# Ten pairs of feed-forward blocks as two-by-two block products with seven multiplications, summed in HBM

## The chip, the cores and the metric

One core of one Trainium2 chip runs the kernel. Its engines are PE (TensorE, the matrix products), DVE (VectorE), ACT (ScalarE), POOL (GpSimd) and SP (SyncE, which here only issues DMAs); each works through its own list of instructions in order and waits on semaphores. PE reads from SBUF and writes into PSUM, which has eight banks of 128 x 512 floats here. The metric is the device time of one launch in microseconds. Before the change it is 2099.76 us, the median of three runs that lie between 2098.71 and 2101.66 us.

## The reference, cut to what matters

The layer holds 1024 tokens of 1024 features, in float32:

```python
x = LN1(ALPHA * x + 0.5 * swiglu(x, f1_gate, f1_up, f1_down))     # feed-forward 1
x = LN2(ALPHA * x + token_mixer(x))                               # gated delta rule and gated linear attention
x = LN3(ALPHA * x + 0.5 * swiglu(x, f2_gate, f2_up, f2_down))     # feed-forward 2

def swiglu(x, w_gate, w_up, w_down):        # 1024 -> 2816 -> 1024
    return (silu(x @ w_gate) * (x @ w_up)) @ w_down
```

The inner width 2816 makes 22 blocks of 128 features in each feed-forward part. The change concerns ten of the 2 x 11 pairs of such blocks.

## The kernel before, in words

Every float32 operand is kept as two parts, hi and lo (`split`, lines 119 to 121: ACT rounds to hi, DVE subtracts and stores lo), and every product is three matrix products: hi hi, hi lo, lo hi. So a product of a 128 x 128 piece of weights with 512 tokens costs three MATMULs of 512 columns each. Tokens lie transposed in SBUF as tiles `xh` and `xl` [features, tokens], eight per half of the tokens.

The work of a block of 128 features, for one half of 512 tokens: `gate_silu` and `up` (both through `proj`, lines 176 to 187) each run 24 MATMULs into one bank `pa` (8 tiles of features times 3). ACT takes silu of the first, DVE multiplies it with the second, and `split` makes the parts of the hidden values. `down` (lines 189 to 211) multiplies the hidden values of two blocks with the rows of w_down: 6 MATMULs into a bank `pd`, then one DVE instruction (line 210) adds the bank to `acc`, the running sum of the layer in SBUF, which starts as x.

Weights come through `weight`: SP loads 128 x 512 (256 KB) into a raw tile `wr` (5 buffers), and ACT and DVE split it into `wh` and `wl` (6 buffers each). The raw loads run ahead as buffers come free.

The order: feed-forward 1, blocks 0 to 11, both halves of the tokens (`ffn_groups`); then the middle, where the remaining ten blocks of feed-forward 1 and the first eight of feed-forward 2 (one half of the tokens at a time) are fed by a hand-written table (`pull`) between the small steps of the mixer, so that PE always has work; then blocks 8 to 21 of feed-forward 2, both halves, the last four of them half by half with the last layer norm behind them. DMAs are issued by SP alone; POOL only raises to a power and clears tiles.

## Time and profile before

| what | value |
|---|---|
| time, median of three runs | 2099.76 us (2098.71 to 2101.66) |
| span of the profiled execution, first to last instruction | 2097.4 us, so some 2.4 us lie around it |
| granted TensorE clock, mean | 0.999 of full |
| PE busy | 2067.7 us, 99% of the span, 10292 instructions |
| DVE busy | 1284.9 us, 61% |
| ACT busy | 697.2 us, 33% |
| POOL busy | 54.6 us, 3% |
| moved by DMA | 163.03 MB, mean 78 GB/s |

The page gives for each engine its busy time and the number of its instructions; a MATMUL's busy time is its length from issue to the modelled end, and MATMULs overlap, so busy time over count is not the time that one of them adds to the span. A group row gives line, engine, operation, output <- inputs, shapes and count, then total busy time, the mean of one, and the idle time of the engine before them with what ended it. A windows row gives for a stretch of the span the busy time and count of each engine, the granted clock, the share of time in which the 16 DMA engines moved data, and the rate.

### The profile page before, as it was taken

How to read it: one execution, taken by the hardware profiler on the slowest of the kernel's cores; microseconds unless marked ns; L12 is line 12 of the kernel's file. 1: busy time of each engine (PE TensorE's matmuls, PEld its weight loads, DVE VectorE, ACT ScalarE, POOL GpSimd, SP SyncE). 2: the span in 40 equal slices, each digit the busy share in tenths (PEclk: the TensorE clock that was granted, in tenths of full speed). 3: DMA queues.
4: the chain of work that ended last, by engine and by line, in shares of the span. 5: the costliest groups of instructions: out<-in, count | busy, mean ns of one | idle time of the engine just before them, and what ended most of it. 6: DMA issues, size and time to landing. Idle time of an engine off the chain costs nothing.

```text
span 2097.4 us, 27456 instructions
## 1 busy us (share of the span) xinstructions
PE 2067.7 (99%) x10292; PEld 1695.0 (81%) x10292; DVE 1284.9 (61%) x2793; ACT 697.2 (33%) x1395; POOL 54.6 (3%) x87
## 2 busy tenths in 40 slices
PE   9999999999999999999999999999999999999998
PEld 7888888888887787788788777888788888888887
DVE  4434333454678888768899887778755333333456
ACT  5211121123254444434464443343422211112232
POOL 0000000000000000000101000001000000000000
PEclk9999999999999999999999999999999999999999
DMA  8111111122222212222131222122323211111232
GB/s 288 49 55 48 43 55 46 46 97 99 89 93 86 71 56 79 70 69 91 66 111 66 71 76 66 66 71 71 121 96 105 80 46 46 51 40 61 76 106 85
DMA packets 87109, 163.03 MB, mean 78 GB/s; under 512 B 10048, under 2 KB 10560, under 8 KB 86976
## 3 DMA queue, kind: packets, MB, share of 16 engines
q1 hardware_dynamic: 86976, 161.29, 22.9%
q8 instruction: 80, 1.31, 0.3%
q14 instruction: 53, 0.43, 0.1%
HBM read 157.06 MB, written 4.19 MB: 77 GB/s over the span
## 4 chain that ended last, share of the span: by engine, by line
PE 87%; DVE 8%; ACT 2%; issue 2%; POOL 1%; DMA 1%; SPq 0%; DVEq 0%; ACTq 0%; POOLq 0%
PE pa L183 17%; PE pa L184 17%; PE pa L186 17%; PE pd L205 8%; PE pd L206 8%; PE pd L207 8%; PE pm L824 1%; PE pm L422 1%; DVE wl L121 1%; DVE acc L210 1%; DVE acc L264 1%; PE pa L724 1%; DVE xl L121 1%; PE pa L725 1%; PE pa L723 1%
## 5 line engine op out<-in xcount | busy, mean ns | idle before, releaser
L183 PE MATMUL pa<-xh,wh 128*128 128x512 f32 x1808 | 716.6, 397 | 8.7 <-ACT xh L120 5.1
L184 PE MATMUL pa<-xl,wh 128*128 128x512 f32 x1808 | 708.7, 392 | 0.1
L186 PE MATMUL pa<-xh,wl 128*128 128x512 f32 x1792 | 704.3, 393 | 0.0
L121 DVE TENSOR_TENSOR wl<-wr,wh 128x512 fp32r<-128x512 f32 (+1 forms) x489 | 334.1, 686 | 350.9 <-ACT wh L120 340.9
L120 ACT CAST wh<-wr 128x512 fp32r<-128x512 f32 (+1 forms) x489 | 302.6, 621 | 709.5 <-PE pa L184 482.9
L183 PEld LDWEIGHTS pa<-xh,wh 128*128 128x128 f32 x1808 | 340.5, 188 | 80.0 <-ACT xh L120 5.9
L184 PEld LDWEIGHTS pa<-xl,wh 128*128 128x128 f32 x1808 | 340.3, 188 | 68.0 <-DVE xl L121 1.8
L186 PEld LDWEIGHTS pa<-xh,wl 128*128 128x128 f32 x1792 | 337.2, 188 | 67.9
L210 DVE SCALAR_TENSOR_TENSOR acc<-pd,acc 128x512 f32<-128x512 f32 x433 | 293.8, 687 | 125.4 <-PE pd L207 122.0
L205 PE MATMUL pd<-wh,hh 128*128 128x512 f32 x416 | 165.4, 404 | 2.2 <-ACT xf L254 1.4
L206 PE MATMUL pd<-wl,hh 128*128 128x512 f32 x416 | 164.2, 396 | 0.1
L207 PE MATMUL pd<-wh,hl 128*128 128x512 f32 x416 | 162.1, 395 | 0.0
L319 DVE TENSOR_TENSOR xf<-xf,pa 128x512 f32<-128x512 f32 x88 | 60.4, 686 | 165.8 <-PE pa L186 165.8
L206 PE MATMUL pd<-fl,gh 128*128 128x512 f32 (+1 forms) x386 | 150.0, 389 | 0.0
L205 PE MATMUL pd<-fh,gh 128*128 128x512 f32 (+1 forms) x386 | 150.0, 389 | 0.0
L207 PE MATMUL pd<-fh,gl 128*128 128x512 f32 (+1 forms) x386 | 149.8, 388 | 0.0
L205 PEld LDWEIGHTS pd<-wh,hh 128*128 128x128 f32 x416 | 78.1, 188 | 24.2 <-ACT hh L120 5.1
L120 ACT CAST fh<-wr 128x512 fp32r<-128x512 f32 x52 | 32.2, 622 | 195.4 <-PE pd L207 165.6
L207 PEld LDWEIGHTS pd<-wh,hl 128*128 128x128 f32 x416 | 78.1, 188 | 17.7 <-DVE hl L121 2.9
L206 PEld LDWEIGHTS pd<-wl,hh 128*128 128x128 f32 x416 | 78.3, 188 | 13.9 <-DVE wl L121 0.8
L205 PEld LDWEIGHTS pd<-fh,gh 128*128 128x128 f32 x386 | 72.5, 188 | 15.2
L207 PEld LDWEIGHTS pd<-fh,gl 128*128 128x128 f32 x386 | 72.5, 188 | 15.2
(251 smaller groups left out, 1987.5 us busy)
## 6 DMA issues: line engine op xcount, KB each, us to landing
wr<-gu SPq DMA_DIRECT2D x263, 256.0 KB, 2.5
wr<-wd SPq DMA_DIRECT2D x132, 256.0 KB, 2.6
wr<-win SPq DMA_DIRECT2D x116, 256.0 KB, 2.6
wr<-wout SPq DMA_DIRECT2D x32, 256.0 KB, 2.5
acc<-xT SPq DMA_DIRECT2D x16, 256.0 KB, 5.4
acc<-x SPq DMA_DIRECT2D x8, 512.0 KB, 8.7
out_dram<-acc SPq DMA_DIRECT2D x7, 512.0 KB, 2.6
g<-lnrow SPq DMA_DIRECT2D x9, 256.0 KB, 3.4
```

The source lines that it names most:

```text
L120: self.nc.scalar.copy(hi, src)
L121: self.nc.vector.tensor_tensor(lo, src, hi.bitcast(F32), ALU.subtract)
L183: nc.tensor.matmul(ps[:], hi[:, sl], xh[k][:], start=(k == 0), stop=False)
L184: nc.tensor.matmul(ps[:], hi[:, sl], xl[k][:], start=False, stop=(lo is None and k == KB - 1))
L186: nc.tensor.matmul(ps[:], lo[:, sl], xh[k][:], start=False, stop=(k == KB - 1))
L205: nc.tensor.matmul(p, hh[:, sl], wh[:, ds], start=(i == 0), stop=False)
L206: nc.tensor.matmul(p, hh[:, sl], wl[:, ds], start=False, stop=False)
L207: nc.tensor.matmul(p, hl[:, sl], wh[:, ds], start=False, stop=(i == n - 1))
L210: nc.vector.scalar_tensor_tensor(acc, p, scale / ALPHA, acc, ALU.mult, ALU.add, accum_out=None if sums is None else sums[:, d:d + 1])
L264: nc.vector.tensor_tensor(acc, acc, g[:], ALU.mult)
L319: self.nc.vector.tensor_tensor(s[:], s[:], ps[:], ALU.mult)
L422: self.nc.tensor.transpose(self.chunk(ps, c), s, self.ident)
```

## The change

Two blocks of features are taken together and all 1024 tokens at once, so that gate, up and down are each a product of matrices cut into two-by-two blocks. Such a product is formed from seven block products instead of eight (with the fewest additions: four sums on each of the two operand sides, and sums of results). In the diff P1 and P2 use plain blocks, P4 uses one plain and one summed block, P3 one summed token block and a plain weight block, and P5, P6, P7 use sums on both sides. Blocks 2 to 11 of feed-forward 1 (five pairs) and blocks 8 to 17 of feed-forward 2 (five pairs) go this way.

- `token_sums` makes the four sums of the tokens once for each chain of five pairs; `weight_sums` makes four sums of the weights for every step (gate, up or down of a pair). Sums are DVE instructions, and each of the seven operands of a step is split into hi and lo.
- `project` runs gate or up: seven products of 12 MATMULs, in two banks that each go on adding; banks that are needed later as partial sums are copied to SBUF by ACT (`keep`).
- `down_sums` runs down: seven products of four tiles of tokens, 12 MATMULs each, in all eight banks. The results don't go to `acc`: ACT copies a bank to a tile `ev` (7 buffers), for P2 and P7 DVE adds the second bank to it, and POOL issues a DMA that adds the tile to the running sum `accd`, which lies in HBM (`add_out`). Twenty such DMAs of 256 KB leave each down step; `out=True` gives `down` the same way out.
- The steps follow each other as gate of pair n+1, down of pair n, up of pair n+1. Weights are prepared four to five products ahead (`DEEP`).
- Because the sum lies in HBM while these chains run, x is first copied there, and `acc` is loaded before the middle, stored behind it and loaded again before the last four blocks. Room in SBUF is given out by phase. The second half of the tokens of blocks 0 to 7 of feed-forward 2 has moved from the end of the middle into the phase behind it, with its sums in HBM too.

On PE there are 8867 rows before and 8507 now, 360 fewer. In the rows below names end in the numbers of their buffers; L595 is ACT's copy of a bank into `ev`, L138 the cast that gives a hi part (`wh` for weights), L510 the copy of a bank in `keep`, L197 POOL's adding DMA, L587 to L589 the products of down, L542 the first product of gate or up. DMASW and DMAHW name landings of POOL's and of SP's DMAs.

DVE, in a down step before: banks are added to the sums in SBUF, and each waits for PE alone.

```order
L210 SCALAR_TENSOR_TENSOR acc0_9_91<-pd_316_1775,acc0_9_91 128x512 [waits PE_49]
L210 SCALAR_TENSOR_TENSOR acc0_9_91<-pd_317_1783,acc0_9_91 128x512 [waits PE_49]
L210 SCALAR_TENSOR_TENSOR acc1_16_110<-pd_318_1791,acc1_16_110 128x512 [waits PE_49]
L210 SCALAR_TENSOR_TENSOR acc1_16_110<-pd_319_1799,acc1_16_110 128x512 [waits PE_49]
L210 SCALAR_TENSOR_TENSOR acc2_21_121<-pd_320_1807,acc2_21_121 128x512 [waits PE_49]
```

ACT now, at the end of a down step (the last tile of P3, then P4's four) and the start of the up step behind it:

```order
L595 ACTIVATE ev_481_1980<-pm_469_1918 128x512 [waits DMASW4_49,DVE_49,PE_49]
L138 CAST wh_488_2012<-wr_471_1924 128x512
L595 ACTIVATE ev_484_1990<-pa_439_1811 128x512 [waits DMASW5_49,DVE_49,PE_49]
L595 ACTIVATE ev_485_1996<-pa_441_1817 128x512 [waits DMASW6_49,DVE_49,PE_49]
L595 ACTIVATE ev_486_2002<-pm_443_1823 128x512 [waits DMASW7_49,DVE_49,PE_49]
L595 ACTIVATE ev_487_2008<-pm_445_1829 128x512 [waits DMASW0_49,PE_49,Activation_49]
L138 CAST wh_492_2031<-wr_472_1926 128x512 [waits DMAHW2_49]
L138 CAST wh_497_2055<-wr_460_1894 128x512 [waits PE_49]
L510 COPY sn_491_2029<-pa_490_2016 128x512 [waits PE_49]
```

Emptying a bank has moved from DVE to ACT, and it now also waits until an earlier adding DMA has landed, since only then is an `ev` tile free. The casts of weights stand behind it in ACT's list.

PE now, at the same place: the last tile of P4, then P1 of the up step.

```order
L587 MATMUL pm_445_1829<-wh_453_1864,xh12_389_1593 128x512 [waits DVE_49]
L588 MATMUL pm_445_1829<-wl_454_1865,xh12_389_1593 128x512
L589 MATMUL pm_445_1829<-wh_453_1864,xl12_390_1594 128x512
L542 MATMUL pa_490_2016<-xh00_7_91,wh_461_1896 128x512 [waits Activation_49]
L543 MATMUL pa_490_2016<-xl00_8_92,wh_461_1896 128x512
L544 MATMUL pa_490_2016<-xh00_7_91,wl_462_1897 128x512
```

P1 of the up step waits for ACT, which has to empty the bank `pa` that P4 filled.

The diff, cut to its core:

```diff
-BUFS = {"w": 6, "h": 3, "xf": 3, "wr": 5, "f": 4, "g": 6, "raw": 1, "q": 1, "k": 2, "v": 1, "tt": 1, "z": 1, "on": 2, "am": 1, "pt": 1, "qd": 1, "vb": 1,
+BUFS = {"w": 6, "h": 3, "xf": 3, "wr": 7, "f": 4, "g": 6, "gs": 4, "sn": 4, "ev": 7, "raw": 1, "q": 1, "k": 2, "v": 1, "tt": 1, "z": 1, "on": 2, "am": 1, "pt": 1, "qd": 1, "vb": 1,
+PRODUCTS = (("P1", 0), ("P2", 1), ("P6", 0), ("P5", 1), ("P7", 0), ("P3", 1), ("P4", 0))
+DEEP = 4
...
+    def load_acc(self, pool):
+        for c in range(KB):
+            self.acc[c] = self.wt(pool, [D], f"acc{c}", 1)
+            self.nc.sync.dma_start(self.acc[c][:], self.accd[c][:])
+    def add_out(self, t, c, d):
+        self.nc.gpsimd.dma_start(self.accd[c][:, HALVES[d]], t[:], accum_op=ALU.add)
...
             for p, (c, d, cut) in zip(ps, now):
+                if out:
+                    t = self.u("ev", self.fx)
+                    nc.scalar.activation(t[:], p, AF.Copy, scale=scale / ALPHA)
+                    self.add_out(t, 4 * half + c, d)
+                    continue
...
+    def token_sums(self, src):
+        tt = self.nc.vector.tensor_tensor
+        self.sx = {n: [] for n in ("P5", "P6", "P7", "P3")}
+        for q in range(KB // 2):
+            a = {}
+            for i, j in ((1, 0), (1, 1), (0, 0), (0, 1)):
+                a[i, j] = self.stage()
+                self.nc.sync.dma_start(a[i, j][:], src(i, 4 * j + q))
+            s1, s2 = self.stage(), self.stage()
+            tt(s1[:], a[1, 0][:], a[1, 1][:], ALU.add)
+            tt(s2[:], s1[:], a[0, 0][:], ALU.subtract)
+            tt(a[0, 0][:], a[0, 0][:], a[1, 0][:], ALU.subtract)
+            tt(a[0, 1][:], a[0, 1][:], s2[:], ALU.subtract)
+            for n, t in (("P6", s2), ("P5", s1), ("P7", a[0, 0]), ("P3", a[0, 1])):
+                hl = [self.wt(self.fx, [HT], f"s{n}{q}{e}", 1, F32R) for e in "hl"]
+                self.split(hl[0][:], hl[1][:], t[:])
+                self.sx[n].append(hl)
...
+    def weight_sums(self, b11, b12, b21, b22):
...
+        t11, t21 = load(b11), load(b21)
+        yield parts(t11)
+        t12, t22 = load(b12), load(b22)
+        yield parts(t21)
+        t2 = self.u("wr", self.wp)
+        tt(t11[:], t12[:], t11[:], ALU.subtract)
+        tt(t2[:], t22[:], t11[:], ALU.subtract)
+        yield parts(t2)
+        yield parts(t11)
+        tt(t12[:], t22[:], t12[:], ALU.subtract)
+        yield parts(t12)
+        yield parts(t22)
+        tt(t21[:], t21[:], t2[:], ALU.subtract)
+        yield parts(t21)
+    def project(self, hid, up):
...
+        for n, b in PRODUCTS:
+            op = yield
+            if n in ("P1", "P2", "P5"):
+                banks[b] = self.bank("pd" if b else "pa")
+            ps = banks[b]
+            for q, (xh, xl) in enumerate(self.tokens(n)):
+                sl = slice(q * P, (q + 1) * P)
+                new = n in ("P1", "P2", "P5") and q == 0
+                nc.tensor.matmul(ps[:], op[0][:, sl], xh[:], start=new, stop=False, skip_group_check=True)
+                nc.tensor.matmul(ps[:], op[0][:, sl], xl[:], start=False, stop=False, skip_group_check=True)
+                nc.tensor.matmul(ps[:], op[1][:, sl], xh[:], start=False, stop=q == 3, skip_group_check=True)
+            if n in ("P1", "P6", "P5"):
+                keep(n, ps)
+            elif n == "P2":
+                done("11", (kept["P1"], ps))
+            elif n == "P7":
+                done("22", (kept["P5"], ps))
+            elif n == "P3":
+                done("12", (kept["P6"], ps))
+            else:
+                done("21", None)
+        if up:
+            s1, s2 = self.u("sn", self.fx), self.u("sn", self.fx)
+            tt(s1[:], hid["21"][:], hid["22"][:], ALU.add)
+            tt(s2[:], s1[:], hid["11"][:], ALU.subtract)
+            tt(hid["21"][:], hid["11"][:], hid["21"][:], ALU.subtract)
+            tt(hid["12"][:], hid["12"][:], s2[:], ALU.subtract)
+            for n, t in (("P6", s2), ("P5", s1), ("P7", hid["21"]), ("P3", hid["12"])):
+                self.hidden_part(hid, n, t)
...
+    def down_sums(self, hid, scale):
+        nc = self.nc
+        tags = ("pa", "pa", "pm", "pm"), ("pd", "pd", "pd", "pm")
+        banks = [[None] * 4, [None] * 4]
+        ev = {}
+        for n, b in PRODUCTS:
+            op = yield
+            hh, hl = hid[n]
+            new = n in ("P1", "P2", "P5")
             for c in range(4):
+                if new:
+                    banks[b][c] = self.bank(tags[b][c])
+                ps, sl = banks[b][c], slice(c * P, (c + 1) * P)
+                nc.tensor.matmul(ps[:], hh[:, sl], op[0][:], start=new, stop=False, skip_group_check=True)
+                nc.tensor.matmul(ps[:], hh[:, sl], op[1][:], start=False, stop=False, skip_group_check=True)
+                nc.tensor.matmul(ps[:], hl[:, sl], op[0][:], start=False, stop=True, skip_group_check=True)
+                if n in ("P2", "P7"):
+                    t = ev[c]
+                    nc.vector.scalar_tensor_tensor(t[:], ps[:], scale, t[:], ALU.mult, ALU.add)
+                else:
+                    t = ev[c] = self.u("ev", self.fx)
+                    nc.scalar.activation(t[:], ps[:], AF.Copy, scale=scale)
+                if n in ("P2", "P6", "P7", "P3", "P4"):
+                    i, j = {"P2": (0, 0), "P6": (0, 1), "P7": (1, 1), "P3": (0, 1), "P4": (1, 0)}[n]
+                    self.add_out(t, 4 * i + c, j)
...
     def run(self):
...
-        self.ffn_groups(1, [range(n, n + 2) for n in range(0, K1, 2)], first=True)
-        with self.tc.tile_pool(name="mp", bufs=1) as self.mp:
-            self.middle()
-        cut = [*range(K2, NF - LAST, 2), NF - LAST]
-        self.ffn_groups(2, [range(a, b) for a, b in zip(cut, cut[1:])], last=range(NF - LAST, NF))
+        self.staged = 0
+        with self.phase("fa") as self.fx:
+            self.scr = "gs", self.fx
+            self.first_pair()
+            self.load_constants()
+            self.token_sums(lambda half, k: self.a["xT"][half, k])
+            self.ffn_pairs(1, range(2, K1))
+        with self.phase("ap") as ap:
+            self.load_acc(ap)
+            with self.phase("hp") as self.hp, self.phase("sp") as self.sp, self.phase("mp") as self.mp:
+                self.scr = "xf", self.hp
+                for k in range(KB // 2):
+                    self.restore(1, k)
+                self.middle()
+            for c in range(KB):
+                self.spill(c, self.acc[c][:])
+        with self.phase("fb") as self.fx:
+            self.scr = "gs", self.fx
+            now(self.ffn(2, range(K2), 1, True))
+            self.token_sums(lambda half, k: self.x2d[half, k][:])
+            self.ffn_pairs(2, range(K2, NF - LAST))
+        self.last_blocks(range(NF - LAST, NF))
...
-        now(self.ffn(2, range(K2), 1))
...
-    nc = bacc.Bacc("TRN2", target_bir_lowering=False, num_devices=1)
+    nc = bacc.Bacc("TRN2", target_bir_lowering=False, num_devices=1, dynamic_dma_scratch_size=4096)
```

More of the change, by code (lines that the diff above doesn't have):

```diff
@@ L96, in __init__ @@
         self.centred = {}
+        self.accd = [None] * KB
+        self.x2d = {}
     def nm(self, s):
@@ L187, in proj, with down @@
         return ps
-    def down(self, hs, ws, half, scale, cs=range(4), sums=None, cuts=((0, HT), (HT, D)), ahead=1):
+    def down(self, hs, ws, half, scale, cs=range(4), sums=None, cuts=((0, HT), (HT, D)), ahead=1, out=False):
         nc = self.nc
@@ L385, in downs_group @@
[L385 to L405 removed]
+            ws = [self.weight(self.a[f"wd{idx}"][f]) for f in fs[i:i + 2]]
@@ new lines, in ffn, with first_pair, last_blocks @@
+            yield from self.down(hs, ws, half, 0.5 if out else 0.25, ahead=AHEAD, out=out)
+    def first_pair(self):
+        hs = [self.hidden_first(self.fx, ("gh", "gl"), 4), now(self.hidden(1, 1, (0, 1), self.fx, ("gh", "gl"), 4))]
+        ws = [self.weight(self.a["wd1"][f]) for f in range(2)]
+        for c in range(KB):
+            self.spill(c, self.a["x"][c])
+        for half in range(2):
+            now(self.down([h[half] for h in hs], ws, half, 0.5, out=True))
+    def last_blocks(self, fs):
+        with self.phase("ep") as fx:
+            self.hp = fx
+            self.scr = "xf", fx
+            self.load_acc(fx)
+            for k in range(KB // 2):
+                self.restore(1, k)
+            for half in range(2):
+                hs = [now(self.hidden(2, f, (half,), fx, ("gh", "gl"), BUFS["g"])) for f in fs]
+                self.last_downs(fs, hs, half, fx)
@@ new lines, in last_downs @@
+    def last_downs(self, fs, hs, half, fx):
+        ws = [self.weight(self.a["wd2"][f], *((fx, "f") if 2 * n < BUFS["f"] else ())) for n, f in enumerate(fs)]
+        for c in range(4):
+            sums = self.wt(self.sl, [2], "sums", 2) if c < 3 else None
+            last = half == 1 and c == 3
+            work = self.down([h[half] for h in hs], ws, half, 0.5, [c], sums,
+                             ((0, HT), (HT, HT + HT // 2), (HT + HT // 2, D)) if last else ((0, HT), (HT, D)))
+            for _ in range(2):
+                next(work)
+            if half or c:
+                self.out_rows(4 * half + c - 1)
+            now(work)
+            self.out_stats(4 * half + c, sums)
+        if half:
+            self.out_rows(KB - 1)
@@ new lines, in ffn_pairs, with add, quarters @@
+    def ffn_pairs(self, idx, fs):
+        gu, wd = self.a[f"gu{idx}"], self.a[f"wd{idx}"]
+        steps, weights, before = [], [], None
+        def add(work, blocks):
+            next(work)
+            steps.append(work)
+            weights.append(self.weight_sums(*blocks))
+        def quarters(m0, m1, rows):
+            q = [m[:, sl] for m in (m0, m1) for sl in HALVES]
+            return (q[0], q[1], q[2], q[3]) if rows else (q[0], q[2], q[1], q[3])
+        for f in range(fs.start, fs.stop, 2):
+            hid = {}
+            add(self.project(hid, False), quarters(gu[f, 0], gu[f + 1, 0], False))
+            if before:
+                add(*before)
+            add(self.project(hid, True), quarters(gu[f, 1], gu[f + 1, 1], False))
+            before = self.down_sums(hid, 0.5 / ALPHA), quarters(wd[f], wd[f + 1], True)
+        add(*before)
+        ops = (op for w in weights for op in w)
+        ready = []
+        for work in steps:
+            for n in range(len(PRODUCTS)):
+                while len(ready) <= DEEP:
+                    op = next(ops, None)
+                    if op is None:
+                        break
+                    ready.append(op)
+                try:
+                    work.send(ready.pop(0))
+                except StopIteration:
+                    assert n == len(PRODUCTS) - 1
```

151 lines of the change are left out of this document (90 added, 61 removed).

## The prediction

> **What bounds the kernel now.** I read the shares of the engines first, then the chain that ended last, then the windows over the two stretches in which only feed-forward blocks run.
>
> ```profile
> PE 2067.7 (99%) x10292; PEld 1695.0 (81%) x10292; DVE 1284.9 (61%) x2793; ACT 697.2 (33%) x1395; POOL 54.6 (3%) x87
> ...
> PE 87%; DVE 8%; ACT 2%; issue 2%; POOL 1%; DMA 1%; SPq 0%; DVEq 0%; ACTq 0%; POOLq 0%
> ```
>
> ```profile
> core 0: us, PE busy (x) PEld busy (x) DVE busy (x) ACT busy (x) POOL busy (x), PEclk, DMA share, GB/s
> 100.00:500.00 400.00, 400.00 (x1762) 330.05 (x1761) 163.37 (x245) 83.05 (x137) 1.08 (x3) 1.00 0.17 58
> 1500.00:1900.00 400.00, 400.00 (x1762) 329.76 (x1761) 169.81 (x255) 92.41 (x152) 0.00 (x0) 1.00 0.21 70
> 0.00:20.00 20.00, 14.86 (x51) 10.89 (x52) 12.25 (x20) 14.94 (x24) 1.38 (x11) 1.00 0.89 320
> 20.00:40.00 20.00, 20.00 (x90) 16.57 (x89) 8.77 (x15) 6.82 (x12) 0.00 (x0) 1.00 0.87 321
> ```
>
> PE is the bound, at a full granted clock, and in the two stretches the change rewrites it never pauses: 1762 MATMULs in 400 us, so one of 512 columns adds 400 / 1762 = 0.227 us. DVE works there for 41% of the time, ACT for 21 to 23%, DMA moves data for 17 to 21%. So fewer MATMULs are time saved, as long as the other engines keep up. The 397 ns of the first row below is the length of one, of which 0.17 us overlap the next.
>
> ```profile
> L183 PE MATMUL pa<-xh,wh 128*128 128x512 f32 x1808 | 716.6, 397 | 8.7 <-ACT xh L120 5.1
> ...
> L120 ACT CAST wh<-wr 128x512 fp32r<-128x512 f32 (+1 forms) x489 | 302.6, 621 | 709.5 <-PE pa L184 482.9
> ...
> L210 DVE SCALAR_TENSOR_TENSOR acc<-pd,acc 128x512 f32<-128x512 f32 x433 | 293.8, 687 | 125.4 <-PE pd L207 122.0
> ```
>
> **The change part by part.** *Removed.* A pair of blocks before: 2 blocks x 2 matrices x 2 halves x 24 MATMULs, and for down 2 halves x 8 banks x 6, 288 in all. Now three steps of seven products of 12: 252. Ten pairs save 360 MATMULs, 360 x 0.227 = **81.7 us**. One step lasts 84 x 0.227 = 19.1 us, a pair 57.2 us where it was 65.4.
>
> *Added on DVE and ACT.* A step splits seven operands where it split four, and makes four sums. For a pair DVE has 21 lo parts and 12 sums of weights, 10 sums and products behind the banks of gate and up, 4 sums and 7 lo parts of hidden values, and 8 additions in down: 62 instructions. ACT has 21 + 7 casts, 10 copies and silus in gate and up, and 20 copies out of down's banks: 58. DVE instructions of this size follow each other every 0.60 us when none waits:
>
> ```profile
> 73.36 0.68 DVE L210 SCALAR_TENSOR_TENSOR acc<-pd,acc 128x512 f32<-128x512 f32 x1
> 73.96 0.68 DVE L121 TENSOR_TENSOR fl<-wr,fh 128x512 fp32r<-128x512 f32 x1
> 74.56 0.68 DVE L210 SCALAR_TENSOR_TENSOR acc<-pd,acc 128x512 f32<-128x512 f32 x1
> 75.16 0.68 DVE L121 TENSOR_TENSOR fl<-wr,fh 128x512 fp32r<-128x512 f32 x1
> ```
>
> 62 x 0.60 = 37 us and 58 x 0.62 = 36 us lie under the 57.2 us of PE; the lead of four to five products (11 to 13 us) covers the up step, whose share on DVE, 29 x 0.60 = 17 us, nearly fills its 19.1. I cost this at nothing; were it not covered, it would show as DVE at 9 tenths.
>
> *Added on DMA, where it is decided.* A down step sends twenty adding DMAs of 256 KB, in bursts of four per product of 2.72 us, through seven `ev` tiles. No trace row shows an adding DMA. The nearest are plain ones:
>
> ```profile
> wr<-gu SPq DMA_DIRECT2D x263, 256.0 KB, 2.5
> ...
> out_dram<-acc SPq DMA_DIRECT2D x2, 256.0 KB, 2.0
> ```
>
> At full load the engines move 320 / 0.89 = 360 GB/s (first window of 20 us) and 321 / 0.87 = 369 (second), so 262144 bytes hold them for 0.73 us; the other 1.8 of the 2.5 us are a fixed way there and back. An addition has to bring two tiles to the adder, `ev` and the old sum, and write one. If reading and writing overlap and both readings do too, it is one pass, **0.73 us**; two readings one behind the other are two passes, **1.46 us**; DMAs that don't overlap at all pay the whole **2.5 us** each. I take two passes, because 360 GB/s is already what the engines read when they do nothing else. The Trainium skill, "Collectives: The Full Stack", section "The bandwidth ceiling: the fold count and why AG ≠ RS ≠ AR", says that an adding transfer reads two sources on one ring and measured 1.93 times a plain one; by it the price would be an estimated 1.41 us and the sum below some 6 us less. No run here shows it yet. POOL's own time for issuing isn't in the trace either; its instructions lie between
>
> ```profile
> L583 POOL TENSOR_TENSOR rk<-rk,mhalf 128x4 f32<-128x4 f32 x8 | 9.9, 1237 | 43.6 <-DVE sa L580 43.6
> ...
> L741 POOL MEMSET q<- 64x512 f32 x4 | 2.1, 521 | 459.6 <-PE pd L207 399.0 <-DVE vb L818 57.4 <-PE pm L422 3.1
> ```
>
> so 0.5 to 1.2 us; I take 0.9, less than the transfer, so that it delays only the first.
>
> *The wait in a down step*, from its first MATMUL (a tile of a product takes 3 x 0.227 = 0.68 us, the step 28 tiles, 19.1 us). P2's first tile is the fifth: 3.4 us, plus 0.17 for the tail, 0.69 on DVE, 0.9 on POOL, 1.8 fixed: 7.0. From then on the queue never runs dry, since the ninth adding DMA (P7's first tile, 17 x 0.68 + 0.9 = 12.4) comes before eight have passed (5.2 + 8 x 1.46 = 16.9). About three of the twelve weight loads of a pair fall in between, 3 x 0.73 = 2.2. The nth lands at 9.2 + 1.46 n: the tenth at 23.8, the thirteenth at 28.2. Of the step's twenty `ev` tiles the seventeenth (P4's first) needs the slot of the tenth, the twentieth that of the thirteenth. So P4's first bank is empty at 23.8 + 0.62 = 24.4 instead of before 19.8. P1 of the up step wants that bank at 19.1: it waits 5.3 us. Then ACT empties P4's fourth bank by 28.2 + 0.62 = 28.8, casts two weights and copies P1 (three times 0.62), 30.7, while PE is through with P1 and P2 at 24.4 + 5.4 = 29.8 and wants to go on adding in P1's bank: 0.9 more. **6.1 us a pair**, in the eight down steps that an up step follows: +49. What queues behind the waiting ACT are the casts of weights, five products ahead, so PE doesn't miss them. The last down step of each chain is followed by a change of phase that wants the memory back, so I count to the twentieth tile, 28.8 - 19.1 = 9.7 us: twice, +19.
>
> *Token sums.* 16 sums and 16 lo parts on DVE, 32 x 0.60 = 19 us, twice, ahead of a gate step whose P1 and P2 (5.4 us) need plain tokens only. Behind the middle, loads of staging tiles also stand behind eight adding DMAs of the block before (12 us, of which some 9 beside PE's work): 19 + 3 - 5.4 = 17. At the start DVE is idle while PE runs 96 MATMULs of the first pair's down (22 us), but half of the staging tiles are `ev` tiles in use: about half of the 19, so 9. Together **+26**.
>
> *Phase changes.* Loading `acc` (4.2 MB, 11.4 us at 369 GB/s) lies under four projections of 24 MATMULs (21.8 us) that don't need it; stores and reloads elsewhere likewise. I take 3 us for seams; without that cover it is 11.
>
> Sum: -81.7 + 49 + 19 + 26 + 3 = +15 on the span of 2097.4, so 2112, and 2115 with the 2.4 us around it (the median shown is 2099.76).
>
> **The rivals.** *An addition costs about one pass.* For it speaks that reading and writing are different directions and the queue is idle for 80% of the time; against it, that 360 to 369 GB/s is reading alone. At 0.73 us the tenth lands at 9.2 + 7.3 = 16.5, the thirteenth at 18.7: no wait in up, none at the chain's end; what stays is 26 + 3, so -52.7: 2044.7 + 2.4 = **2047**, faster. In between the time moves by some 13 x 8 + 13 x 2 = 130 us for 1 us of price, so no change lies at 1.46 - 15 / 130 = 1.34 us.
>
> *Adding DMAs go one at a time*, because each reads, adds and writes before the next does: 2.5 us each, the fixed part within. The tenth lands at 5.2 + 2.2 + 25 = 32.4, P1 starts at 33.0 (13.9 late), P6 waits another 4: 17.9 x 8 = 143; chain ends 2 x 21.4 = 43; token sums 30, seams 3. Sum +137, with the 2.4: **2237**, slower still. It decides from about 2 us up. For it: the fixed 1.8 us is most of a plain DMA; against it: at full load plain DMAs do overlap.
>
> *POOL can't issue beside DVE.* If issuing had to wait for gaps of DVE, busy for 37 of 57 us, 0.9 us would become 0.9 / 0.35 = 2.6 us, and the time much the same as that. The 87 POOL instructions of before say nothing on it. The Trainium skill, "SBUF — State Buffer", section "Who interferes with whom", has DVE's copies in its two-port modes block the writing of descriptors, but says that instructions with two SBUF inputs, which these are, only hold up reading by GpSimd; by that page this rival falls.
>
> *The products aren't saved.* Excluded: the list of PE is 360 rows shorter, all of the 512-column kind.
>
> **How the numbers follow.** Two passes, prices from 1.3 to 2 us: chance 0.54, with a range of its own from 2095 to 2185 (130 us for 1 us of price). One pass, or nearly: 0.32. One at a time or a starved POOL: 0.14. A measurement of this kernel tells 0.2%, 4.2 us, from no change. The band 2095.6 to 2104 holds 0.09 of the first case (prices 1.31 to 1.38); 0.01 of it lies below. So faster 0.33, same 0.09, slower 0.58. The range for 8 in 10 must reach to the one-pass case and leaves about a third of it out below, 2045; above, 2190 leaves out most of the slowest cases.
>
> **What would show it.** Right: PE has 360 fewer MATMULs; adding DMAs follow each other in a down step every 1.4 to 1.5 us; PE pauses 5 to 6 us at P1 of each up step, and ACT's copies into `ev` wait for DMA; two longer pauses lie where the tokens' sums are made. Wrong: no pause at P1 and a distance near 0.73 us (one pass), or pauses of 15 us and POOL busy all through the down step (the slow rivals). PE's pause somewhere else than in front of ACT's copies would break the whole chain of reasons.

## The result and the profile after

The changed kernel takes 2154.42 us (median of 4 runs, 2154.14 to 2156.38), the one before 2100.71 us beside it (2098.71 to 2103.24): a ratio of 1.0255, 95% interval 1.0240 to 1.0269. It is slower, as forecast, but by 54 us where 15 had been forecast. The profiled execution has a span of 2152.5 us, 55.1 more than before.

From the page of the changed kernel (busy times, queue of the adding DMAs, chain of waits, POOL's group, issues):

```profile
PE 2047.5 (95%) x9932; PEld 1641.7 (76%) x9932; DVE 1439.8 (67%) x3069; ACT 955.4 (44%) x1863; POOL 272.9 (13%) x335
...
q0 software_dynamic: 35712, 65.03, 17.8%
...
PE 55%; issue 23%; POOL 7%; DVE 7%; DMA 5%; ACT 2%; POOLq 0%; SPq 0%; DVEq 0%; ACTq 0%
...
L197 POOL DMA_DIRECT2D accd<-ev x248 | 218.2, 1320 | 730.4 <-DVE ev L592 449.6
...
accd<-ev POOLq DMA_DIRECT2D x248, 256.0 KB, 8.5
```

PE has its 360 MATMULs less (10292 to 9932), but its share fell from 99% to 95% and its part of the chain from 87% to 55%; "issue" (time in which the profile shows no wait) has 23% there now, POOL 7% and DMA 5%. The packets of the 248 adding DMAs add up to 17.8% of the span on 16 engines, 0.178 x 2152.5 / 248 = 1.54 us each. But packets of adding DMAs overlap: from 289.64 to 297.33 us, where no weight load comes between, they add up to more than the whole time of the engines, and ACT, which waits there for one landing after the other, starts every 1.28 us:

```profile
q0 software_dynamic: 855, 1.56, 112.1%
...
292.31 0.60 ACT L595 ACTIVATE ev<-pd 128x512 f32<-128x512 f32 x1 [0.68 <-DMA accd<-ev]
293.59 0.60 ACT L595 ACTIVATE ev<-pm 128x512 f32<-128x512 f32 x1 [0.69 <-DMA accd<-ev]
...
296.16 0.60 ACT L595 ACTIVATE ev<-pd 128x512 f32<-128x512 f32 x1 [0.44 <-DMA accd<-ev]
297.44 0.60 ACT L595 ACTIVATE ev<-pd 128x512 f32<-128x512 f32 x1 [0.68 <-DMA accd<-ev]
```

So an adding DMA takes **1.28 us of the queue**, where 1.46 had been taken. POOL needs 218.2 / 248 = 0.88 us for an issue, where 0.9 had been taken. From issue to landing the median is 8.5 us, since they queue.

The windows of the changed kernel over the two chains of pairs, over the two stretches with the token sums, and over two pieces of the chains:

```profile
core 0: us, PE busy (x) PEld busy (x) DVE busy (x) ACT busy (x) POOL busy (x), PEclk, DMA share, GB/s
100.00:400.00 300.00, 280.31 (x1171) 221.69 (x1170) 187.71 (x301) 155.19 (x276) 74.70 (x87) 0.98 0.57 121
1700.00:2000.00 300.00, 278.80 (x1149) 218.56 (x1147) 180.88 (x288) 150.49 (x267) 79.45 (x90) 0.97 0.60 125
60.00:120.00 60.00, 52.23 (x208) 40.10 (x208) 33.05 (x53) 30.23 (x51) 11.21 (x13) 0.91 0.62 139
1650.00:1710.00 60.00, 45.41 (x168) 33.99 (x167) 38.12 (x61) 28.10 (x49) 6.98 (x8) 0.80 0.50 132
220.00:300.00 80.00, 74.24 (x303) 58.03 (x301) 45.75 (x73) 40.43 (x72) 26.51 (x32) 0.96 0.71 141
1750.00:1830.00 80.00, 70.78 (x286) 54.74 (x285) 42.90 (x69) 39.78 (x70) 25.62 (x29) 0.95 0.70 141
```

Before, 400 us of such a chain held 400 us of PE and 1762 MATMULs, 1321 in 300 us; now it is 1171 and 1149. PE stands idle for 20 us in 300, and the granted clock, 1.00 before, is 0.98 and 0.97. The two stretches of the token sums are the worst: 208 and 168 MATMULs where 60 us held 264.

One pair's seam, from the timeline of the changed kernel (start, length, what; in brackets the idle time before it). The four ACTIVATEs empty P4's four banks, COPY sn<-pa is the copy of P1's bank in the up step:

```profile
301.09 0.60 ACT L595 ACTIVATE ev<-pa 128x512 f32<-128x512 f32 x1 [0.72 <-DVE wl L139]
301.74 0.50 PE L542 MATMUL pa<-xh,wh 128*128 128x512 f32 x1 [3.32 <-ACT ev L595]
304.14 0.60 ACT L595 ACTIVATE ev<-pa 128x512 f32<-128x512 f32 x1 [2.46 <-DMA accd<-ev]
305.53 0.60 ACT L595 ACTIVATE ev<-pm 128x512 f32<-128x512 f32 x1 [0.79 <-DMA accd<-ev]
306.79 0.60 ACT L595 ACTIVATE ev<-pm 128x512 f32<-128x512 f32 x1 [0.66 <-DMA accd<-ev]
307.29 1.13 ACT L138 CAST wh<-wr 128x512 fp32r<-128x512 f32 x2
308.31 0.59 ACT L510 COPY sn<-pa 128x512 f32<-128x512 f32 x1
308.95 0.50 PE L542 MATMUL pa<-sP60h,wh 128*128 128x512 f32 x1 [1.48 <-ACT sn L510]
```

That is the forecast's picture, instruction by instruction: P1 of the up step (301.74) starts when P4's first bank is empty, ACT waits for landings every 1.3 to 1.4 us (3.05 where packets of weight loads come between, sent at 295 to 298 us), and P6 (308.95) waits a second time because ACT copies P1's bank only behind P4's fourth and two casts.

The starts of the MATMULs divide the 55.1 us by stage. The first pair takes 71.2 us (69.4 before), the first chain 341.8 (326.7), the middle with what belongs to it 1239.1 (1230.3), the second chain 353.6 (326.7), the last stage 134.1 (131.6). So 42 of the 55 lie in the chains, which were to become 82 us shorter. The experiments ask what fills them.

### The profile page after: what moved, and what is told of

The parts are those of the page before. It is cut to its first block, busy times and chain, and to the rows that moved or that the text cites. A ratio compares the mean times of both kernels' runs of the same rounds, so it can differ in the third digit from the quotient of the medians.

```text
span 2152.5 us, 28629 instructions
## 1 busy us (share of the span) xinstructions
PE 2047.5 (95%) x9932; PEld 1641.7 (76%) x9932; DVE 1439.8 (67%) x3069; ACT 955.4 (44%) x1863; POOL 272.9 (13%) x335
## 3 DMA queue, kind: packets, MB, share of 16 engines
q0 software_dynamic: 35712, 65.03, 17.8%
q8 instruction: 78, 1.28, 0.2%
## 4 chain that ended last, share of the span: by engine, by line
PE 55%; issue 23%; POOL 7%; DVE 7%; DMA 5%; ACT 2%; POOLq 0%; SPq 0%; DVEq 0%; ACTq 0%
PE pa L207 10%; PE pa L208 9%; PE pa L210 9%; POOL accd L197 7%; PE pd L230 4%; PE pd L229 4%; PE pd L231 4%; DMA accd<-ev 4%; PE pm L1054 1%; PE pm L652 1%; DVE wl L139 1%; PE pa L544 1%; PE pa L542 1%; PE pa L543 1%; DVE acc L239 1%
## 5 line engine op out<-in xcount | busy, mean ns | idle before, releaser
L139 DVE TENSOR_TENSOR wl<-wr,wh 128x512 fp32r<-128x512 f32 (+1 forms) x623 | 423.8, 686 | 375.0 <-ACT wh L138 365.7
L138 ACT CAST wh<-wr 128x512 fp32r<-128x512 f32 (+1 forms) x623 | 383.2, 620 | 607.7 <-PE pa L208 304.9
L207 PE MATMUL pa<-xh,wh 128*128 128x512 f32 x1168 | 469.6, 402 | 14.6 <-ACT ev L595 5.7
L208 PE MATMUL pa<-xl,wh 128*128 128x512 f32 x1168 | 461.6, 395 | 0.1
L210 PE MATMUL pa<-xh,wl 128*128 128x512 f32 x1152 | 456.1, 396 | 0.0
L197 POOL DMA_DIRECT2D accd<-ev x248 | 218.2, 1320 | 730.4 <-DVE ev L592 449.6
L207 PEld LDWEIGHTS pa<-xh,wh 128*128 128x128 f32 x1168 | 221.0, 189 | 63.1 <-ACT ev L595 6.6
L208 PEld LDWEIGHTS pa<-xl,wh 128*128 128x128 f32 x1168 | 221.0, 189 | 43.2 <-DVE xl L139 1.8
L210 PEld LDWEIGHTS pa<-xh,wl 128*128 128x128 f32 x1152 | 217.5, 189 | 43.4
L239 DVE SCALAR_TENSOR_TENSOR acc<-pd,acc 128x512 f32<-128x512 f32 (+1 forms) x225 | 150.6, 683 | 29.0 <-PE pd L231 26.6
L542 PE MATMUL pa<-xh,wh 128*128 128x512 f32 x160 | 69.1, 432 | 26.3 <-ACT ev L595 26.3
L544 PE MATMUL pa<-xh,wl 128*128 128x512 f32 x160 | 68.3, 427 | 5.1 <-DVE wl L139 5.1
L543 PE MATMUL pa<-xl,wh 128*128 128x512 f32 x160 | 67.8, 424 | 0.0
L595 ACT ACTIVATE ev<-pm 128x512 f32<-128x512 f32 x80 | 46.7, 599 | 46.9 <-DMA accd<-ev 43.2
L542 PEld LDWEIGHTS pa<-xh,wh 128*128 128x128 f32 x160 | 33.3, 208 | 37.3 <-ACT ev L595 29.7
L595 ACT ACTIVATE ev<-pd 128x512 f32<-128x512 f32 x60 | 35.8, 598 | 45.9 <-DMA accd<-ev 42.3
```

The lines of the kernel that those rows point to most:

```text
L138: self.nc.scalar.copy(hi, src)
L139: self.nc.vector.tensor_tensor(lo, src, hi.bitcast(F32), ALU.subtract)
L197: self.nc.gpsimd.dma_start(self.accd[c][:, HALVES[d]], t[:], accum_op=ALU.add)
L207: nc.tensor.matmul(ps[:], hi[:, sl], xh[k][:], start=(k == 0), stop=False)
L208: nc.tensor.matmul(ps[:], hi[:, sl], xl[k][:], start=False, stop=(lo is None and k == KB - 1))
L210: nc.tensor.matmul(ps[:], lo[:, sl], xh[k][:], start=False, stop=(k == KB - 1))
```

## The experiments

At first I held that the missing 40 us were the granted clock: behind PE's pauses the trace shows it at half speed for 3.4 to 24 us at a time, which no term of the forecast contains. Against this stood the price of the addition, the number of ev tiles, and the token sums.

**The addition itself.** Plain stores instead of adding ones, from the same queue:

```diff
-        self.nc.gpsimd.dma_start(self.accd[c][:, HALVES[d]], t[:], accum_op=ALU.add)
+        self.nc.gpsimd.dma_start(self.accd[c][:, HALVES[d]], t[:])
```

> The blocks' results go to HBM from the same queue by the same issues, but as plain stores, without the addition (so what lies in HBM is the last block's result, not the sum). Theory (the price of the addition, two passes, holds the ev tiles): a 2 KB packet falls from 178 to about 84 ns, the transfer of 256 KB from about 1.45 to 0.75 us, the pauses of 3 to 4.5 us at P1 of the up steps go and the half-speed stretches of the clock behind them too; eight pairs lose 67 us less and the two last down steps some 10 to 20: 2060 to 2085. Rival (POOL's issue of 0.87 us and the way of a transfer to its landing set the pace, not the addition): the pauses stay and the time is 2140 to 2155.

Measured: 2065.25 us. From the page and the windows (columns as above) of this kernel:

```profile
q0 software_dynamic: 19840, 65.03, 8.5%
...
accd<-ev POOLq DMA_DIRECT2D x248, 256.0 KB, 4.2
```

```profile
150.00:340.00 190.00, 190.00 (x822) 153.99 (x821) 124.94 (x199) 109.68 (x194) 39.75 (x75) 1.00 0.46 158
60.00:120.00 60.00, 55.74 (x229) 43.28 (x228) 35.89 (x58) 32.08 (x54) 6.93 (x13) 0.97 0.41 142
1610.00:1670.00 60.00, 48.77 (x188) 37.17 (x187) 42.37 (x69) 28.09 (x48) 1.93 (x4) 0.86 0.38 125
```

The packets of the same 65.03 MB add up to 0.085 x 2063.4 / 248 = 0.71 us a transfer, so the adding one is 1.54 / 0.71 = 2.2 times as dear; by the landings in the two traces, 1.28 us where adding DMAs follow closely and 0.62 where plain ones do, 2.1 times. 89 us hang on it. The edit takes away two things at once, the addition and half of the data packets (plain ones carry 4 KB, adding ones 2 KB); which of them is the price isn't parted. PE has no pause left inside the chains. The theory on the addition holds. POOL's path as the cause falls too, though not by this run alone, in which an issue also went from 0.88 to 0.54 us: in the changed kernel POOL could issue every 0.88 us, and landings in a row come every 1.28. (The Trainium skill, "Collectives: The Full Stack", section "The bandwidth ceiling: the fold count and why AG ≠ RS ≠ AR", has a measured ratio of 1.93 between the rates of a collective that only copies and of one that adds; measured here, 2.1 to 2.2.) But the windows show three things more. The token sums still cost 8.4 + 18.1 = 26.5 us, just the 26 of the forecast; the changed kernel pays 13.2 + 22.6 = 35.8, so over 9 us of them come from adding DMAs. (In both, some 2 us are the pace of the MATMULs told of below and not the sums.) And with PE busy for all of 190 us, 822 MATMULs make 0.231 us each, not the 0.227 of before.

**The number of ev tiles.** Five or eight instead of seven:

```diff
-... "sn": 4, "ev": 7, ...
+... "sn": 4, "ev": 5, ...
```

> Five ev tiles in place of seven; nothing else is changed. Theory (P4's evictions wait for a slot that an earlier adding DMA still reads): P4's first eviction waits for the twelfth adding DMA instead of the tenth, two transfers of 1.45 us later, so 2.9 us more in each of eight pairs and two chain ends, +29, with the clock's answer to longer pauses up to +45: 2175 to 2200. Rival (the pause is the queue's or POOL's own pace, with no part of the slots): 2154 to 2160.

> Eight ev tiles in place of seven; nothing else is changed. Theory (P4's first eviction waits for the slot of the tenth adding DMA with seven tiles; five tiles cost 4.4 us more a down step): with eight it waits for the ninth, one transfer or a transfer and a weight load earlier, 1.5 to 2.2 us less in eight pairs and two chain ends, so 2134 to 2142. Rival (at seven the slots are no longer what ends last, but ACT's own row of copies and casts): 2150 to 2155.

Measured: 2199.10 us with five (2193.74 and 2204.45), 2133.83 with eight (1.0156 of before, 1.0139 to 1.0173). The waits, in us in total, times and the longest, of the kernel with five, of the changed kernel with its seven and of that with eight:

```profile
ACT ev L595 <- DMA accd<-ev: 132.8, 134, 3.2
...
PE pa L542 <- ACT ev L595: 46.8, 8, 6.8
```

```profile
ACT ev L595 <- DMA accd<-ev: 118.0, 110, 3.6
...
PE pa L542 <- ACT ev L595: 26.3, 8, 4.4
```

```profile
ACT ev L595 <- DMA accd<-ev: 87.3, 93, 2.2
...
PE pa L542 <- ACT ev L595: 20.9, 8, 3.5
```

A down step with the wait behind it lasts 29.0 us with five tiles, 24.4 with seven, 22.4 with eight: 2.0 to 2.3 us for a tile, one adding DMA with its share of weight loads. The mechanism of the forecast is shown: P4's eviction waits for a slot that a DMA still reads. Eight tiles also save 4 us in the token sums, about half of whose staging tiles are `ev` tiles; of the gain, 7 us are lost again in the last stage (141.2 for 134.1).

**The clock.** Sixteen MATMULs into a spare bank ahead of P1 of each up step, so that PE does not pause there:

```diff
+            if n == "P1" and up:
+                idle = self.bank("pd")
+                for r in range(FILL):
+                    nc.tensor.matmul(idle[:], op[0][:, 0:P], self.xh[0][0][:], start=True, stop=True)
```

> Sixteen MATMULs whose result nobody reads stand on PE ahead of P1 of each up step, where it pauses for 3 to 4.5 us; 16 x 0.227 = 3.6 us. Theory (behind such a pause the granted clock falls to half for 3.4 to 6.8 us, some 41 us in the two chains, so up to 20 us are lost to the clock and not to the pause): the clock stays at 1.00 in the chains outside the token sums, and the time falls by 10 to 18 us to 2136 to 2144 though PE does 36 us more work. Rival (only the pauses cost): no gain, 2154 to 2162, since the sixteen fill a little more than the shortest pauses.

Measured: 2154.31 us, ratio 1.0255 (1.0238 to 1.0272), the changed kernel's to the last digit. The windows of this kernel over the two pieces shown above:

```profile
220.00:300.00 80.00, 77.41 (x328) 60.74 (x327) 44.82 (x71) 40.55 (x72) 26.83 (x32) 1.00 0.72 141
1750.00:1830.00 80.00, 77.01 (x325) 60.23 (x325) 44.64 (x71) 39.82 (x71) 26.68 (x31) 1.00 0.71 141
```

The clock stays at 1.00 over these pieces, where it was 0.96 and 0.95 (in the eight seams 3.4 us at half speed remain of 30.6), and nothing is gained. My theory falls. What the slow clock stretched were P1 and P2 of the up step, and behind them P6 waits for ACT anyway: at full speed PE arrives earlier and waits longer (1.2 to 2.0 us at P6 instead of 0 to 1.6). The sixteen of the two first up steps fell into the pauses for the token sums, so the run tells of those too:

```profile
60.00:120.00 60.00, 54.93 (x228) 43.51 (x227) 33.73 (x55) 30.44 (x52) 10.37 (x12) 0.97 0.61 141
1650.00:1710.00 60.00, 47.75 (x187) 36.69 (x186) 37.66 (x62) 28.51 (x49) 6.98 (x8) 0.89 0.49 132
```

The clock rose from 0.91 to 0.97 and from 0.80 to 0.89, but without the sixteen only 4 and 3 MATMULs more fit into the 60 us, about 1 us each.

The Trainium skill, "TensorE: Matmul & The Clock Gate", section "HAM oscillation — how this bites in real kernels", counts half of the slow time as lost; 30.6 us of it lie in the eight pairs, so by that rule an estimated 15 us. The trace agrees that the clock falls to half behind pauses (in six of the eight seams, at pauses of 2.9 to 4.4 us), but the price here was about 1 us: from their first down step to the last the pairs took 485.3 us with the filling and 486.6 without. In these seams ACT's copy of P1's bank ended last, or nearly so, and not PE.

**The token sums.** Left out, with plain tokens in their place (this changes what is computed):

```diff
-... .get(n, lambda: self.sx[n])()
+... .get(n, lambda: x(0, 0))()
-            self.token_sums(lambda half, k: self.a["xT"][half, k])
-            self.token_sums(lambda half, k: self.x2d[half, k][:])
```

> The sums of the tokens and their parts are not made; the four products that use them read plain tokens (so the result is another). Theory (the pauses and half-speed stretches at 81 to 100 us and 1662 to 1689 us are the token sums, 35.8 us against the 26 of the forecast): both go, 2118 (2112 to 2124). Rival (the forecast's 26 was right and the rest of these stretches belongs to the change of phase and the block ahead of it): 2128 or more, with a half-speed stretch left behind 1662 us.

Measured: 2123.46 us. The two steps behind the sums last 57.2 and 56.9 us instead of 70.4 and 79.6, which is the bare work of 252 MATMULs, so the sums, with the pace of the MATMULs that read them, cost all of the 35.8; of the gain, 6 us are lost again in the last stage (140.2 for 134.1).

Made in smaller groups and earlier:

```diff
-        for c in range(KB):
-            self.spill(c, self.a["x"][c])
+        for half in range(2):
+            for c in range(4 * half, 4 * half + 4):
+                self.spill(c, self.a["x"][c])
         for half in range(2):
+            self.token_sums(lambda i, k: self.a["xT"][i, k], range(2 * half, 2 * half + 2))
...
-            now(self.ffn(2, range(K2), 1, True))
-            self.token_sums(lambda half, k: self.x2d[half, k][:])
+            for q in range(KB // 2):
+                now(self.ffn(2, range(2 * q, 2 * q + 2), 1, True))
+                if q < 3:
+                    for r in ((0, 1), (2,), (3,))[q]:
+                        self.token_sums(lambda half, k: self.x2d[half, k][:], range(r, r + 1))
```

> The four groups of token sums are made one by one beside the blocks ahead of the pairs (two ahead of each half of the first pair's down; at the second chain behind the first three pairs of the block by block part) instead of all at once in front of the gate step. Theory (the 33 us of pauses there are DVE's 32 instructions in a row, on which PE waits): 25 to 32 us less, 2122 to 2130, and the granted clock stays at 1.00 around 85 and 1670 us. Rival (the sums' loads and staging tiles stand behind adding DMAs, so the wait only moves ahead into the downs): 2140 to 2155.

Measured: 2141.48 us, ratio 1.0202 (1.0185 to 1.0219), 13 us less and not 25 to 32. Windows of this kernel:

```profile
1650.00:1710.00 60.00, 60.00 (x260) 48.56 (x260) 35.79 (x57) 28.99 (x51) 6.98 (x8) 1.00 0.39 88
1500.00:1650.00 150.00, 142.34 (x606) 113.61 (x605) 79.94 (x126) 65.09 (x112) 21.02 (x24) 0.99 0.70 192
```

The second hole is closed (260 MATMULs for 168), but 44 MATMULs are missing in the 150 us ahead, which held 650 in the changed kernel; the first pair now takes 82.4 us instead of 71.2, and the last stage 140.0 instead of 134.1. So the rival was right that the wait moves ahead. Of SP's waits, first in the changed kernel from 60 to 120 us, then in the changed kernel and in this one from 1500 to 1660:

```profile
SPq L458 <- DMA accd<-ev: 12.7, 5, 5.6
```

```profile
SPq L458 <- DMA accd<-ev: 4.7, 2, 3.8
```

```profile
SPq L461 <- DMA accd<-ev: 17.1, 9, 2.4
```

The loads of the sums (L458, now L461) wait on SP for staging tiles that adding DMAs still read, and weights stand behind them in SP's list. That late weights are what PE then lacks isn't shown.

**The pace of the MATMULs.** By the built program's placement, the tiles of the phases start 32 bytes beyond a multiple of 64, and 416 bytes apart from the tiles of tokens and weights when only the place within 2 KB is counted. The 48 MATMULs of P6, P5, P7 and P3 in a gate step are slow in the plain-store kernel too, and always the same ones. A tile of 8 numbers (32 bytes), and in a second kernel of 408 (1632 bytes), ahead of the phases' pools moves them:

```diff
         self.sl = pool("sl", 1)
+        pad = self.sl.tile([P, 8], F32, name="pad")
+        self.nc.gpsimd.memset(pad[:, 0:8], 0.0)
```

> A tile of 32 bytes is put ahead of the pools of the phases, so that every 2 KB tile in them starts at a multiple of 64 bytes instead of 32 beyond one; no instruction of the blocks is changed. Theory (a MATMUL that streams from a tile 32 bytes beyond a multiple of 64 takes 231 to 237 ns to the next instead of 227, seen in the tiles of the tokens' sums, of the hidden parts and of the middle's hidden parts): all go at 227, some 0.8 to 1.2 us less in each pair, 5 to 6 in the middle, 1 to 2 behind: 2138 to 2147. Rival (the slower pace comes from more traffic of DVE, ACT and DMA in the SBUF, not from where the tiles lie): 2150 to 2157 with the pace unchanged.

> The tile put ahead of the phases' pools is 1632 bytes instead of 32, so that their 2 KB tiles start at the same place within 2 KB (1152) as the tiles of the tokens and of the weights. Theory (a MATMUL whose two operands stand at different places within 2 KB takes longer to the next: 416 bytes apart most at 231 to 237 ns, 448 apart some, 32 apart in the kernel before few, 0 apart none): all 512-column MATMULs of the pairs and the middle go at 227 ns, and the time is 2136 to 2146. Rival (the multiple of 64 was all there is in the place): 2148 to 2152, as with 32 bytes, and the products of the tokens' sums stay at 231 to 237 ns.

Measured: 2150.13 us with 32 bytes (1.0237, 1.0221 to 1.0252, not told apart from the changed kernel), 2140.80 with 1632 (1.0197, 1.0181 to 1.0212). The first and the last of those 48 MATMULs in one gate step (start, length), in the timeline of the changed kernel and in that of the kernel with 1632 bytes:

```profile
328.45 0.40 PE L542 MATMUL pa<-sP60h,wh 128*128 128x512 f32 x1
...
339.46 0.40 PE L544 MATMUL pd<-sP33h,wl 128*128 128x512 f32 x1
```

```profile
324.67 0.39 PE L544 MATMUL pa<-sP60h,wh 128*128 128x512 f32 x1
...
335.32 0.39 PE L546 MATMUL pd<-sP33h,wl 128*128 128x512 f32 x1
```

11.01 us for 47 steps against 10.65: **0.2343 us apart against 0.2266**. So the multiple of 64 was not it. With the phases' tiles at the same place within 2 KB as the tokens and weights the slow pace is gone, and some 13 us of the time with it.

That the distance between a MATMUL's own two operands is all of it isn't shown. In the last stage of the changed kernel fifteen groups of six MATMULs (`pd<-fh,gh` and the like) read both operands from the phases' tiles, so at distance 0, and they too are 0.231 to 0.232 us apart; with 1632 bytes all but one of these groups are at 0.2266. In the kernel before, the same kind goes at 0.2269 in runs of 96, and at 0.231 to 0.232 in groups of six between MATMULs whose operands lie 32 bytes apart. So the neighbours may count as well.

**Fewer adding DMAs.** P6's copy stays in an sn tile, P3's bank is added to it by DVE, and a down step sends sixteen instead of twenty:

```diff
+                elif n == "P6":
+                    part[c] = self.u("sn", self.fx)
+                    nc.scalar.activation(part[c][:], ps[:], AF.Copy, scale=scale)
+                elif n == "P3":
+                    t = part[c]
+                    nc.vector.scalar_tensor_tensor(t[:], ps[:], scale, t[:], ALU.mult, ALU.add)
...
-                if n in ("P2", "P6", "P7", "P3", "P4"):
+                if n in ("P2", "P7", "P3", "P4"):
```

> P6's copy out of the banks is kept in an sn tile and P3's result is added to it by DVE, so that a down step sends sixteen adding DMAs instead of twenty and P4's evictions take the ev slots of P2's, which are long free. Theory (the pairs wait for ev slots held by adding DMAs): the pauses at P1 and P6 of the up steps go, 7 us in each of eight pairs, and most of the 9 us at each of two chain ends: 2075 to 2095. Rival (DVE, with 66 instructions a pair, 40 us of 57, or the up step's copies into sn tiles that DMAs still read, takes over): pauses at P6 of the up step of over 3 us, 2110 or more.

Measured: 2095.81 us, ratio 0.9978, 0.9969 to 0.9988: 0.2% faster than before and 59 us faster than the changed kernel. The edit does two things, four adding DMAs fewer and four copies that no longer take an `ev` tile, and the run doesn't part them. The pause at P1 is gone (a down step lasts 19.5 us, as with plain stores); at P6 0.5 to 1.5 us stay, in total

```profile
PE pa L542 <- ACT sn L510: 2.7, 4, 1.1
```

over the four pairs of the first chain. DVE does not take over.

**All of it together**, that is the sixteen adding DMAs, the early token sums and the moved tiles; first as above with 32 bytes, then with the token sums made in place from four tiles a group, each with its own load, and 1632 bytes:

> The three together: sixteen adding DMAs, the token sums early, tiles at multiples of 64 bytes. Theory (the three losses are separate places): before less the 81.7 us of the MATMULs saved plus chain ends and seams of 10 to 25: 2030 to 2050, faster than before and than each alone. Rival (one bound stands behind the others, DVE or the DMA engines): 2070 or more.

> Sixteen adding DMAs and the 1632 bytes, with the token sums made in place from four tiles a group (the tags sn, ev and gs by name), so that no load of theirs waits on SP for a tile that an adding DMA still reads; at the second chain the loads go out a pair of blocks ahead of the sums. Theory (the version with early token sums lost some 8 us at 1528 to 1602 us and 4 at 71 because SP and DVE waited there for staging tiles, and weights stood behind them): 2045 to 2062. Rival (DVE is simply full there): 2068 to 2078, as the three together before.

Measured: 2073.55 us (0.9871, 0.9856 to 0.9886) and 2069.89 (0.9864, 0.9848 to 0.9880). Each is better than the kernel before, and each misses what its theory expected. In the second the steps behind the token sums lose nothing more (57.1 and 56.9 us), but the middle, in which the second sums are made now, takes 1246.9 us instead of 1239.1, and the last stage is 146.9 us long. PE's waits from 1900 to 1940 us there and SP's from 1880 to 1940:

```profile
PE pa L209 <- ACT xf L348: 13.2, 1, 13.2
```

```profile
SPq L196 <- DMA accd<-sn: 7.2, 2, 5.6
SPq L196 <- DMA accd<-ev: 7.0, 4, 2.3
```

The loads of acc (L196) wait on SP for the last adding DMAs. So the loads were moved behind the first blocks' weights, and in a second version two of P4's four evictions went from ACT to DVE:

```diff
-            self.load_acc(fx)
+            self.late = [(fx, range(4)), (fx, range(4, KB))]
...
                 hs.append(h[half])
+                if self.late:
+                    self.load_acc()
```

> As the kernel with token sums in place and the 1632 bytes, but the loads of acc from HBM at the two chain ends stand on SP behind the weights of the first block of the next phase (four tiles) and of its second (four), not ahead of all of them. Theory (at the chain ends these loads wait on SP for the last adding DMAs, and weights and tokens behind them come late: 13 us of pause at 1920 us, 4 at 396): 2049 to 2058, with the last stage back at 132 to 135 us from 147. Rival (the phase's own memory is what comes late, whatever the order on SP): 2064 or more.

> As the one before, and two of P4's four evictions are done by DVE instead of ACT. Theory (the pauses of 0.6 to 2.2 us at P6 of each up step are ACT's row of four evictions, casts and P1's copy): they shrink by 0.6 to 1.2 us, 5 to 10 us in all, 2042 to 2052. Rival (DVE, busy two thirds of the time there, makes its additions and lo parts later by as much): no gain, 2050 to 2062.

Measured: **2060.03 us** (0.9804, 0.9790 to 0.9819) and 2070.13 (0.9852, 0.9837 to 0.9866). The first is 2 us above what its theory expected. The order on SP was a part of it: the last stage falls from 146.9 to 140.9 us, not to 135. A pause of 8.2 us stays (waits of the kernel with the loads moved, from 1925 to 1952 us):

```profile
PE pa L210 <- ACT xf L349: 8.2, 1, 8.2
...
ACT fh L140 <- DMA wr<-wd: 14.3, 1, 14.3
```

ACT's copy, for which PE waits, stands in ACT's list behind the cast of a piece of w_down, and this waits for its load, which SP issues from 1937.77 us on, behind the eight loads of acc (from 1930.52). So it is the order on SP once more.

The second, 10 us slower, lies outside both of its expectations. Sharing P4's evictions helped nothing, so the theory on ACT's row falls: P6's waits in the first chain went from 1.8 to 3.0 us in total (kernel with the loads moved, then the shared one),

```profile
PE pa L558 <- ACT sn L526: 1.8, 3, 0.7
```

```profile
PE pa L558 <- ACT sn L526: 3.0, 4, 1.0
```

and the pause behind the first chain grew from 3.8 to 9.6 us, while ACT waited there for the first weights of the middle (12.3 us instead of 8.8). Why these come later isn't known.

## Why the prediction was right in its sign and short by 40 us

The likeliest case was the one that came: two passes for an addition, a wait for ev slots, slower. Its 2115 us were wrong all the same. Its terms against the stages of the changed kernel, all in us:

| term | forecast | measured | from |
|---|---|---|---|
| 360 MATMULs less | -81.7 | -81.7 | at 0.227 each |
| wait of a down step, eight pairs | +49 | +58 | changed kernel less plain stores, 7.3 a pair |
| two last downs | +19 | +20 | 29.0 + 29.6 less 2 x 19.1 |
| token sums | +26 | +36 | 70.4 + 79.6 less 114.2 |
| seams | +3 | +13 | first pair 1.8, middle 8.8, last stage 2.5 |
| pace of the MATMULs | none | +10 | plain stores: 58.4 a pair for 57.2, eight pairs |
| sum | +15 | +55 | |

*Right:* POOL's 0.9 (0.88), the place where it is decided, the order of the two waits at P1 and P6, and that DVE and ACT stay under PE's work. Five, seven and eight ev tiles moved the time as the slots require. The rival of one pass was priced at 2047; the plain stores, which are one pass, gave 2065, the difference being pace, seams and 4 us in the two last downs. The starved POOL fell with the 0.88 us, one at a time with the 1.28.

*Right by luck, the tenth landing:* 23.8 us after the start of a down step were forecast, and the mean over the eight steps is 23.7. But an adding DMA takes 1.28 us of the queue and not 1.46, while the first lands at 9.7 us and not at 7.0 + 1.46 = 8.5, and weight loads come in between. With 1.28 alone put right, the forecast's own 130 us for 1 us of price would have made +15 into -8, slightly faster.

*Mis-sized, the step "6.1 us a pair":* 7.3. P1's part was forecast as 5.3 and is 4.9 (the pause alone, forecast as 5 to 6, is 2.9 to 4.4); P6's was 0.9, and the up and gate steps are 2.4 us longer than with plain stores. From P4's first eviction to its fourth it takes 5.7 us in the seam shown (301.09 to 306.79), not 4.4, with packets of weight loads between the landings; the thirteenth lands at 29.6 us (mean of the eight), not at 28.2.

*Mis-sized, the step "token sums":* the work of DVE was about right, 26 us remain with plain stores, some 2 of them pace. The 9 us more are staging tiles that adding DMAs hold. The forecast knew of that hold and counted it too low: 9 us in the first chain, where 13.2 came, and 17 in the second, where 22.6 came.

*Missing, the pace:* "one of 512 columns adds 0.227 us" was read from a kernel whose tiles lay otherwise. The change moved tiles, and more than half of the pairs' MATMULs became 2 to 4% slower. A number of the trace of before was taken for one of the instruction, when it also belonged to the placement. Where PE waits for DMA anyway, as in the down steps, this cost nothing; in gate and up steps and in the token sums it did.

*Mis-sized, the seams:* 13 for 3. The first pair, the middle and the last stage hold no changed instruction but the loads and stores at their edges. That the loads of acc stand on SP behind adding DMAs is shown only for faster versions. For the middle's 8.8 us I have no cause: with 1632 bytes 7.0 of them stay, with plain stores 6.3.

*What I believed after the first look and what fell:* that the clock was the missing term. The one run on it shows that the half-speed stretches inside the pairs cost about 1 us, and those at the token sums, cut by the same run from 34.1 to 17.1 us in all, gave back about 1 us for each chain.

## What to carry to other kernels

A wait that a trace names is the one that ends last, and so a slower clock, or a slower MATMUL, in front of it may be free: before a term is added for it, ask what the engine would have waited for next. An accumulating DMA is paid twice, in its transfer and in the tile that it holds until it lands; here four additions of twenty moved to an engine with time to spare, and to other tiles, were worth more (59 us) than any other single edit that keeps the result. A rewrite that moves tiles can change the pace of the instructions that it leaves alone, so the unit price read before should be read again after.

## What the runs showed of the hardware that was not expected

- The place of a MATMUL's operand tiles matters: 0.2343 us apart when they stand 416 bytes apart within 2 KB, 0.2333 at 448, 0.2266 at 0 (the same 48 MATMULs of a gate step). Why, and at which distances, stays open, and MATMULs of the last stage at 0 are slow too (0.231 to 0.232) where their neighbours are not at 0.
- Adding DMAs of 256 KB in a row land every 1.28 us and plain ones from the same queue every 0.62 (their packets add up to 1.54 and 0.71 us on each of the 16 engines), and POOL is busy for 0.88 us with the one and 133.4 / 248 = 0.54 us with the other, whose 65.03 MB went out in 19840 packets instead of 35712:

```profile
L197 POOL DMA_DIRECT2D accd<-ev x248 | 133.4, 541 | 724.6 <-DVE ev L592 433.7
```

- A pause of PE of some 3 us can halve the granted clock for 3.4 or 6.8 us (PEclk 0.96 over 80 us with one such stretch of 6.8), at a cost of about 1 us for 30.6 us of half speed where another engine is late behind it.
